# Two output tiles of a streamed projection by turns in two PSUM banks, and the pacing in groups of six

## The chip, the cores and the metric

One core of one Trainium2 chip runs the whole program. The metric is device time in microseconds (us). TensorE (PE in the profile) multiplies, VectorE (DVE) and ScalarE (ACT) do the element-wise work, GpSimd (POOL) does a few small things, SyncE (SP) starts most of the transfers.

## The reference

One block of a hybrid model, 512 tokens by 1024 features in float32. A normalized input is projected once, and three mixers (a gated linear recurrence, a delta-rule recurrence, attention) read parts of that projection. Their gated outputs are summed, projected, and a feed-forward layer follows.

```python
h = rms_norm(x, mix_pre_g)
z = h @ w_in                                   # [512, 11200]
zq, zf, zi, zog, zrw, zcq, zckv, zkr, zgate = split(z)
o_hg, o_rw, o_mla = hgrn2(zq, zf, zi, zog), rwkv7(zrw), mla(zcq, zckv, zkr)
g_hg, g_rw, g_mla = split(sigmoid(zgate), 3)
merged = g_hg * (o_hg @ w_branch[0]) + g_rw * (o_rw @ w_branch[1]) + g_mla * (o_mla @ w_branch[2])
x = x + rms_norm(merged @ w_out, mix_post_g)
gate, up = split(rms_norm(x, ffn_pre_g) @ w_ffn_in, 2)
x = x + rms_norm((silu(gate) * up) @ w_ffn_out, ffn_post_g)
```

## The kernel before

**Products in three parts.** Every float32 operand of a large product is split into a high part, rounded to fp32r, and the low part that is left over. A product of two such operands is three matmuls into one PSUM place: high by high (L136, `whD` and `xH`), high weights by low operand (L137, `whD` and `xL`), low weights by high operand (L138, `wlD` and `xH`). `mm3` issues the three.

**Streamed projections.** `stream` makes two output tiles of 128 features by 512 tokens at a time from 256 columns of weights. The weights come in four slabs of two k-tiles each: a transfer to `wsD` (L200), a cast to `whD` on ACT (L204) and a subtraction to `wlD` on DVE (L131 through L205). `whD` and `wlD` have two places each, so a slab's cast waits until the slab two before it has been read for the last time. For each slab the kernel before takes the first output tile with both k-tiles (six matmuls), then the second. Each output tile has one PSUM bank, under the tag `mmD`. In the first 1,020 us the pool of these banks has two places; in the feed-forward layer it has four. A finished tile is read out by `done`: by ACT to `zst` (L236 for the projection, L250 for the gates), by DVE to `th` in the branches (L1104), by ACT and DVE in the feed-forward layer (L1200, L1201, L1205). The next stream's tile can be begun in a bank only when that has been read out.

**What else runs on TensorE.** Up to about 1,020 us the streams are work that fills TensorE's time between the products of the mixers: `pr` (preparation of the delta-rule recurrence), `zus` and `yb` (its steps and their inverses), `ph` (the gated recurrence), `pm`, `pmt`, `pmo` (attention). Those are float32 products without the split, small ones mostly, and each waits for results of DVE, ACT or POOL. `side_by_side` issues products on different rows of the array one after the other; its first product stands at L190, the others at L193, and each of these is only handed out once the one before it has been issued. From 1,020 us on there is only filling work: the output projection and the feed-forward layer (`po` and again `mmD`).

**The order.** A scheduler lays down the order of each engine's instructions when the program is built. `lane(n)` gives what follows a priority: a lower lane goes first when its operands are ready. Each engine then takes its instructions strictly in this order and waits at each for what it needs.

**Pacing.** `pace` (L140) is told the first and the last matmul of a group. It puts a memset of a one-element tile, `token` (L148), on POOL behind the last one, and makes the first matmul of a group wait for the token of the group PACE before. With groups of three and PACE = 5, at most 15 filling matmuls stand in front of a product of a recurrence.

Of the kernel before, what the change touches and what calls it, by code (L numbers as in the profile page):

```python
# [23 lines left out]
S = 512  # L24
# [17 lines left out]
PACE = 5  # L42
SCALE = 192.0 ** -0.5

# columns of the constants array
# [10 lines left out]
def consts_array():  # L56
    """Constants that the shapes alone decide."""
# [15 lines left out]
def masks_array():  # L73
    """Pairs (s, t), both in one block of HB, in the left and the right half of one block of 2m"""
    i, j = np.arange(P) % HB, np.arange(HB)
    c = np.zeros((P, len(HG_LEVELS), HB), np.float32)
    for n, m in enumerate(HG_LEVELS):
        same = (i[:, None] // (2 * m)) == (j[None, :] // (2 * m))
        c[:, n, :] = same & ((i[:, None] // m) % 2 == 0) & ((j[None, :] // m) % 2 == 1)
    return c  # L80


# rows of the table of per-feature vectors: name, rows of 128
# [13 lines left out]
def vecs_array(inputs):  # L97
    """The per-feature vectors side by side, features on partitions"""
# [3 lines left out]
class Kern:  # L102
# [7 lines left out]
    def lane(self, n):  # L110
        """What follows is issued before what is ready in later lanes."""
# [17 lines left out]
    def split_low(self, dst, src, high, eng=None):  # L129
        """The part of src that rounding it to high left over."""  # L130
        (eng or self.nc.vector).tensor_tensor(dst, src, high.bitcast(F32), op=ALU.subtract)  # L131

    def mm3(self, ps, lh, ll, rh, rl, start, stop):
        """One tile of a float32 product from operands that are split exactly in two."""
# [5 lines left out]
    def pace(self, first, last):  # L140
        """Holds back the products that fill the array's time until those PACE groups before are
        done, so that what a recurrence waits for doesn't queue behind many of them."""
# [10 lines left out]
    def load_w(self, pool, src, kts, n, tag, bufs=None, step=None):  # L153
        """Loads a slab [128, kts, n] of weights in parts of `step` k-tiles and splits it; gives a
        function that gives the parts of k-tile k."""
# [18 lines left out]
    def operand(self):  # L174
        """The 16 tiles of a feature-major operand of 1024 features, in two parts"""
        return [[self.t(self.hp, [P, S], f"x{a}{k}", F32R) for k in range(KD)] for a in "HL"]

    def stream_open(self, es):
        """Places of the weights that run through"""
# [5 lines left out]
    def side_by_side(self, calls):  # L185
        """Products on different rows or columns of the array, issued in this order"""
# [8 lines left out]
    def slab(self, src, pool=None, hold=None):  # L195
        """A part [128, kts, n] (2 KB a partition) of weights, split"""
# [12 lines left out]
    def stream(self, src, x, done, toks=slice(0, S), ps=None):  # L209
        """Feature-major products of up to 256 columns of weights; done(j, ps) takes the tiles."""  # L210
# [4 lines left out]
        for k0 in range(0, KD, 2):  # L215
            h, l = self.slab(src[:, k0:k0 + 2])
            for c, p in zip(cols, ps):
                for k in range(2):
                    group = self.mm3(p[:c.stop - c.start, toks], h[:, k, c], l[:, k, c], xh[k0 + k][:, toks],
                                     xl[k0 + k][:, toks], k0 + k == 0, k0 + k == KD - 1)  # L220
                    if self.pacing:
                        self.pace(*group)
# [8 lines left out]
    def dense_z(self, off, n=256, halves=False):  # L231
        """A part of the input projection, feature-major, to DRAM; in halves of the tokens"""
# [13 lines left out]
    def dense_gate(self, n):  # L246
        """Two tiles of tanh of half the gates' logits, to DRAM"""
# [6 lines left out]
    def dense_fm(self, ps, w, x, kts, col=0, toks=slice(0, S)):  # L254
        """ps[feature, token] = sum over kts of w[k][:, feature]^T x[:, k, token]"""
# [6 lines left out]
    def dense_tm(self, ps, w, x, kts, tt, cols):  # L262
        """ps[token, feature] = sum over kts of x[:, kt, token]^T w[:, kt, feature]"""
# [7 lines left out]
    def rstd(self, dst, ss, n, eps, tmp):  # L271
        """dst = (ss / n + eps) ** -0.5"""
# [58 lines left out]
    def to_fm(self, sp, pp, xs, gname, groups, first=False):  # L331
        """Row-normalizes token tiles and lays them out feature-major, in two parts."""
# [25 lines left out]
    def derived(self, sp):  # L358
        """Per-feature vectors that the inputs give."""
# [22 lines left out]
        # lower bound: softmax over the single layer, cumulative sum less the first  # L382
# [25 lines left out]
    def shifted(self, dst, j):  # L408
        """dst = token shift of the recurrence's input tile j"""
# [23 lines left out]
    def rwkv_group(self, g):  # L433
        """Four heads: what the recurrence needs, the inverses, the recurrence"""
# [45 lines left out]
    def rwkv_prep(self, G, p, q):  # L480
# [8 lines left out]
        # decays, from the chunk's end: ep = exp(c - c_end), em its inverse  # L489
        lh, ll = self.lora_w(((H[0], ins["rwkv_w_up"][0, :, f]), (H[1], ins["rwkv_a_up"][0, :, f])))  # L490

        # the two halves of the rows side by side in the array
# [25 lines left out]
        # normalized keys  # L518
# [24 lines left out]
        # in-context learning rates: a = 2 * rate - 1  # L543
# [13 lines left out]
        # scores  # L557
# [16 lines left out]
        # [b|k] token-major  # L574
# [6 lines left out]
        # bonus  # L581
# [7 lines left out]
        # gate  # L589
# [6 lines left out]
        # values, token-major  # L596
# [9 lines left out]
    def rwkv_inverse(self, G, g):  # L606
        """T = (I - L)^-1 for the chunks' strictly lower triangular L, in blocks of 32"""
# [5 lines left out]
        # transposed and in place  # L613
# [17 lines left out]
    def rwkv_merge(self, G, g):  # L631
        """The inverses' blocks off the diagonal"""
# [22 lines left out]
    def rwkv_chain(self, G, g, between):  # L655
# [10 lines left out]
        for c in range(NC):  # L666
# [5 lines left out]
            if 0 < c < NC - 1:  # L672
                # the state as it comes to the end of the next chunk
# [27 lines left out]
        # layer norm over the head  # L701
# [12 lines left out]
        for q in range(2):  # L714
# [9 lines left out]
            for j in range(2):  # L724
                # odd heads have the two chunks of a tile in the other order
# [9 lines left out]
    def hgrn_open(self, es):  # L735
# [3 lines left out]
        # what lies above the diagonal's blocks stays zero  # L739
# [8 lines left out]
    def hgrn_head(self, h):  # L748
# [5 lines left out]
        # decays and keys  # L754
# [8 lines left out]
        # values, token-major  # L763
# [6 lines left out]
        # output gate, doubled  # L770
# [6 lines left out]
        # scores [s, t] inside tiles of 128 tokens: the diagonal first, then pairs whose tokens  # L777
        # lie in the left and right half of a block of 2m, with the decay up to the middle in q
        # and from there on in k; those inside blocks of HB in their own tile at first
# [530 lines left out]
```

## Time and profile before

| | |
|---|---|
| median of 3 runs | 1442.45 us (1441.33 to 1442.66) |
| the profiled execution, first to last instruction | 1441.5 us |
| TensorE busy | 1410.8 us, 9,832 matmuls |
| matmuls of `stream` | 3 x 1,232 and 3 x 64 |
| VectorE, ScalarE, GpSimd busy | 872.7, 631.7, 154.4 us |
| DMA | 194.94 MB, 135 GB/s |

The profile is of one execution; its span lies 0.95 us under the median. Matmuls overlap, and the duration in a row of a matmul holds its way through the array: a 128x512 matmul of 390 ns is followed by the next one 227 ns later. So what a matmul costs TensorE is read from the distance of two starts, not from its duration. A timeline's columns are: start, duration, engine, line, operation, tiles (out<-in), shape, count, and in brackets how long the engine had been idle and for whom. Rows with a count hold several instructions. Lines are those of the kernel before.

### The profile page before, as it was taken

Reading aid. Unit: us, or ns where it says so; the run is one execution under the profiler, and the core shown is the slowest. Engines: PE = TensorE matmul, PEld = TensorE weight load, DVE = VectorE, ACT = ScalarE, POOL = GpSimd, SP = SyncE. Lnnn points to the kernel's source line nnn. Section 1 sums busy time; section 2 is a strip of 40 time slices with the busy share of each in tenths; the row PEclk is TensorE's granted clock in tenths of the full one; section 3 lists DMA queues with packets and bytes.
Section 4 is the critical chain, followed back from the end, with each engine's and each line's share of the span. In section 5 each row is a group of like instructions: output and inputs, shape, how many; then the busy total and the mean of one; then the engine's idle time right before and its main releaser. Section 6 shows DMA issues by size and latency. Waiting matters only on the chain.

```text
span 1441.5 us, 27838 instructions
## 1 busy us (share of the span) xinstructions
PE 1410.8 (98%) x9832; PEld 1116.7 (77%) x9832; DVE 872.7 (61%) x1910; ACT 631.7 (44%) x1266; POOL 154.4 (11%) x1027
## 2 busy tenths in 40 slices
PE   7999999999999999999999999999999999999998
PEld 6777777777777777777877787887788888888886
DVE  5657967867689496874835666655465444443234
ACT  5563555544646346335543455333354333332222
POOL 2110111110212121111111010001010000000000
PEclk9999999999999999999999999999999999999999
DMA  6455453444544444445532456435544333335333
GB/s 204 141 172 153 132 162 98 140 140 132 171 136 142 125 133 133 129 104 173 153 107 78 141 163 183 137 115 177 198 153 139 99 99 96 95 97 159 95 95 110
DMA packets 172459, 194.94 MB, mean 135 GB/s; under 512 B 33056, under 2 KB 125600, under 8 KB 172320
## 3 DMA queue, kind: packets, MB, share of 16 engines
q1 hardware_dynamic: 170928, 190.02, 43.9%
q10 hardware_dynamic: 1392, 3.15, 0.6%
q8 instruction: 78, 1.28, 0.4%
q14 instruction: 61, 0.50, 0.1%
HBM read 151.30 MB, written 41.81 MB: 134 GB/s over the span
## 4 chain that ended last, share of the span: by engine, by line
PE 88%; DMA 5%; DVE 3%; ACT 2%; issue 1%; SPq 0%; POOL 0%; DVEq 0%; POOLq 0%; ACTq 0%
PE mmD L136 19%; PE mmD L138 18%; PE mmD L137 18%; PE po L136 4%; PE po L138 4%; PE po L137 4%; PE pr L193 2%; PE ph L786 1%; DMA zr<-z 1%; PE yb L697 1%; PE pmo L1082 1%; DMA z<-zst 1%; PE pm L136 1%; PE pm L138 1%; PE pm L137 1%
## 5 line engine op out<-in xcount | busy, mean ns | idle before, releaser
L136 PE MATMUL mmD<-xH,whD 128*128 128x512 f32 (+1 forms) x1232 | 489.9, 399 | 5.8 <-ACT whD L204 3.1
L137 PE MATMUL mmD<-xL,whD 128*128 128x512 f32 (+1 forms) x1232 | 474.1, 386 | 0.0
L138 PE MATMUL mmD<-xH,wlD 128*128 128x512 f32 (+1 forms) x1232 | 453.4, 388 | 2.9 <-DVE wlD L131 2.8
L131 DVE TENSOR_TENSOR wlD<-wsD,whD 128x512 fp32r<-128x512 f32 x384 | 263.5, 687 | 306.0 <-ACT whD L204 294.5
L204 ACT CAST whD<-wsD 128x512 fp32r<-128x512 f32 x384 | 237.5, 619 | 454.6 <-PE mmD L137 290.2
L136 PEld LDWEIGHTS mmD<-xH,whD 128*128 128x128 f32 x1232 | 231.5, 188 | 59.2 <-POOL token L148 5.6
L138 PEld LDWEIGHTS mmD<-xH,wlD 128*128 128x128 f32 x1232 | 230.4, 188 | 52.6 <-DVE wlD L131 5.5
L137 PEld LDWEIGHTS mmD<-xL,whD 128*128 128x128 f32 x1232 | 232.4, 189 | 40.9 <-issue 0.9
L148 POOL MEMSET token<- 1x1 f32 x912 | 82.8, 91 | 786.2 <-PE mmD L138 769.6
L138 PE MATMUL po<-whD,fL 128*128 128x512 f32 x176 | 68.3, 390 | 0.0
L137 PE MATMUL po<-wlD,fH 128*128 128x512 f32 x176 | 68.3, 390 | 0.0
L136 PE MATMUL po<-whD,fH 128*128 128x512 f32 x176 | 50.9, 391 | 0.2
L278 POOL TENSOR_TENSOR rrs<-rtm,mhalf 128x1 f32<-128x1 f32 x8 | 4.7, 589 | 405.2 <-DVE rtm L273 368.0
L236 ACT COPY zst<-mmD 128x512 f32<-128x512 f32 x64 | 37.5, 585 | 21.3 <-PE mmD L138 20.9
L621 DVE TENSOR_TENSOR invtmp<-inv 64x30 f32<-64x30 f32 (+14 forms) x120 | 38.8, 323 | 10.2 <-DMA inv<-Ld 7.9
L622 DVE TENSOR_TENSOR inv<-inv,invtmp 64x30 f32<-64x30 f32 (+14 forms) x120 | 38.3, 319 | 1.9
L136 PEld LDWEIGHTS po<-whD,fH 128*128 128x128 f32 x176 | 32.9, 188 | 8.0 <-DVE y L1177 0.6
L138 PEld LDWEIGHTS po<-whD,fL 128*128 128x128 f32 x176 | 33.0, 188 | 7.1
L137 PEld LDWEIGHTS po<-wlD,fH 128*128 128x128 f32 x176 | 33.0, 188 | 7.0
L695 DVE SCALAR_TENSOR_TENSOR PV<-zus,gC,St 64x64 f32<-64x64 f32 x96 | 27.1, 282 | 10.5 <-PE zus L689 7.2
L786 PEld LDWEIGHTS ph<-hq,hk 128*32 128x32 f32 x1536 | 19.5, 111 | 12.6 <-issue 5.4
L786 PE MATMUL ph<-hq,hk 128*32 128x32 f32 x1536 | 27.4, 200 | 0.3 <-DVE hq L791 0.3
(335 smaller groups left out, 2009.0 us busy)
## 6 DMA issues: line engine op xcount, KB each, us to landing
wsD<-in_w_in_dram SPq DMA_DIRECT2D x176, 256.0 KB, 3.0
wsD<-in_w_ffn_in_dram SPq DMA_DIRECT2D x96, 256.0 KB, 2.8
z<-zst SPq DMA_DIRECT2D x63, 256.0 KB, 2.6
wsD<-in_w_branch_dram SPq DMA_DIRECT2D x48, 256.0 KB, 2.7
wsD<-in_w_ffn_out_dram SPq DMA_DIRECT2D x44, 256.0 KB, 2.6
zr<-z SPq DMA_DIRECT2D x26, 256.0 KB, 3.1
gth<-zst SPq DMA_DIRECT2D x24, 256.0 KB, 2.1
th<-gth SPq DMA_DIRECT2D x24, 256.0 KB, 3.6
```

The costliest lines, as they stand in the source:

```text
L131: (eng or self.nc.vector).tensor_tensor(dst, src, high.bitcast(F32), op=ALU.subtract)
L136: first = mm(ps, lhsT=lh, rhs=rh, start=start, stop=False)
L137: mm(ps, lhsT=lh, rhs=rl, start=False, stop=False)
L138: return first, mm(ps, lhsT=ll, rhs=rh, start=False, stop=stop)
L148: token = self.nc.gpsimd.memset(self.token, 0.0).ins
L193: last = c()
L204: nc.scalar.copy(h, st)
L236: self.nc.scalar.copy(st[:m], ps)
L621: V.tensor_tensor(tv, cv, rv, op=ALU.mult)
L622: V.tensor_tensor(U[:, :j, j + 1:], U[:, :j, j + 1:], tv, op=ALU.add)
L695: V.scalar_tensor_tensor(nxt, zus[H[e], 2, q, :], gc, St[H[e], q, :], op0=ALU.mult, op1=ALU.add)
L786: mm(g[b:b + HB, o // P, :], lhsT=k[:, t], rhs=q[:, t], start=True, stop=True)
```

## The change

In `stream` the loops change places: k-tile by k-tile, and within a k-tile the three kinds of product one after the other, each for both output tiles before the next kind. A group of the pacing is now these six matmuls (two banks, three products), and PACE is 3, so that up to 18 of them stand in front of a recurrence, and half as many tokens are made. `stream` issues its matmuls itself, at L222, and no longer through `mm3`. Comments and docstrings were dropped; what stands below `stream` moves down by three lines (L236 is L239, L786 is L789, L1104 is L1107).

```diff
-PACE = 5
+PACE = 3
...
         for k0 in range(0, KD, 2):
             h, l = self.slab(src[:, k0:k0 + 2])
-            for c, p in zip(cols, ps):
-                for k in range(2):
-                    group = self.mm3(p[:c.stop - c.start, toks], h[:, k, c], l[:, k, c], xh[k0 + k][:, toks],
-                                     xl[k0 + k][:, toks], k0 + k == 0, k0 + k == KD - 1)
-                    if self.pacing:
-                        self.pace(*group)
+            for k in range(2):
+                a, b, i = xh[k0 + k][:, toks], xl[k0 + k][:, toks], k0 + k
+                out = [p[:c.stop - c.start, toks] for c, p in zip(cols, ps)]
+
+                made = [nc.tensor.matmul(o, lhsT=w[:, k, c], rhs=x, start=i == 0 and n == 0, stop=i == KD - 1 and n == 2)
+                        for n, (w, x) in enumerate(((h, a), (h, b), (l, a))) for c, o in zip(cols, out)]
+                if self.pacing:
+                    self.pace(made[0], made[-1])
```

The scheduler lays the order down anew, and it moves more than these lines. Numbers behind a tile's name tell places apart; they differ between the two programs (`mmD_1029` before stands where `mmD_965` stands now).

TensorE, at a product of the delta-rule recurrence (`pr`, the scores of one pair of heads, eight products side by side) within a stream. Before:

```order
L138 MATMUL mmD_1029<-xH_7_106,wlD_1034 128x512
L190 MATMUL pr_4924<-X_775_4679,BK_4907 128x128
L136 MATMUL mmD_1029<-xH_8_107,whD_1055 128x512
L137 MATMUL mmD_1029<-xL_16_115,whD_1055 128x512
L193 MATMUL pr_4925<-X_776_4680,BK_4907 128x128
L193 MATMUL pr_4924<-X_775_4679,BK_4907 128x128
L193 MATMUL pr_4925<-X_776_4680,BK_4907 128x128
```

And now the same eight products:

```order
L222 MATMUL mmD_966<-xL_18_117,whD_1009 128x512
L770 MATMUL ph_7411<-cst,hz_7409 128x128
L789 MATMUL ph_7424<-hq_7407,hk_7401 32x32 x16
L190 MATMUL pr_4564<-X_775_4319,BK_4547 128x128
L193 MATMUL pr_4565<-X_776_4320,BK_4547 128x128
L193 MATMUL pr_4564<-X_775_4319,BK_4547 128x128
L193 MATMUL pr_4565<-X_776_4320,BK_4547 128x128
```

The first of the eight stood alone between filling matmuls, and two of these ran before the other seven; now the eight follow one another, behind products of the gated recurrence. Counted over the whole order, a first product (L190) stood alone in this way 17 times before and stands so twice now. Unbroken stretches of other work between filling matmuls were 293 and are 253.

TensorE, where one stream of the last branch ends and the next begins (no mixer has work left there). Before:

```order
L138 MATMUL mmD_12062<-oH_1809_10879,wlD_12133 128x512
L136 MATMUL mmD_12063<-oH_1808_10878,whD_12132 128x512
L137 MATMUL mmD_12063<-oL_1816_10886,whD_12132 128x512
L138 MATMUL mmD_12063<-oH_1808_10878,wlD_12133 128x512
L136 MATMUL mmD_12063<-oH_1809_10879,whD_12132 128x512
L137 MATMUL mmD_12063<-oL_1817_10887,whD_12132 128x512
L138 MATMUL mmD_12063<-oH_1809_10879,wlD_12133 128x512
L136 MATMUL mmD_12168<-oH_1802_10872,whD_12172 128x512
```

And now:

```order
L222 MATMUL mmD_11631<-oH_1809_10455,wlD_11695 128x512
L222 MATMUL mmD_11630<-oH_1809_10455,whD_11694 128x512
L222 MATMUL mmD_11630<-oL_1817_10463,whD_11694 128x512
L222 MATMUL mmD_11630<-oH_1809_10455,wlD_11695 128x512
L222 MATMUL mmD_11728<-oH_1802_10448,whD_11732 128x512
L222 MATMUL mmD_11728<-oL_1810_10456,whD_11732 128x512
```

`mmD_12168` and `mmD_11728` are begun in the bank of `mmD_12062` and `mmD_11630`. Six matmuls stood between the last one into the old tile and the first into the new one; now none stands there. At the other ends of streams mostly one filling matmul stands there, where mostly four or six did, and with it whatever of the mixers the scheduler found ready; at six of the 55 ends in the first 1,020 us that is nothing.

ACT, where the fourth stream ends and the fifth begins. Before (`whD_707` is the cast of the fourth stream's last slab, `whD_739` and `whD_761` those of the next stream's first two slabs):

```order
L204 CAST whD_707<-wsD_705 128x512
L204 CAST whD_739<-wsD_737 128x512
L236 COPY zst_727<-mmD_637 128x512
L204 CAST whD_761<-wsD_759 128x512
L236 COPY zst_731<-mmD_638 128x512
```

And now (`whD_669` is the last slab, `whD_699` and `whD_719` the next stream's first two):

```order
L204 CAST whD_669<-wsD_667 128x512
L204 CAST whD_699<-wsD_697 128x512
L552 ACTIVATE a_4346<-a_4346,omka,hka 128x512
L204 CAST whD_719<-wsD_717 128x512
L239 COPY zst_687<-mmD_605 128x512
L239 COPY zst_691<-mmD_606 128x512
```

The copy of the first output tile stood ahead of the cast of the next stream's second slab; now it stands behind it, and that cast takes the place of the old stream's last slab, which TensorE reads until two matmuls before the end. It is so at 43 of the 44 ends of streams that ACT reads out.

More of the change, by code (lines that the diff above doesn't have):

```diff
@@ L209, in stream @@
     def stream(self, src, x, done, toks=slice(0, S), ps=None):
+        nc = self.nc
         xh, xl = x
```

## The prediction

> **What bounds the kernel now.** I read the page first, then what TensorE's matmuls cost by the distance of their starts, then the places where TensorE changes between filling matmuls and a mixer's products, then the ends of the streams.
>
> The page's first part, its chain of waits, and one of the three groups of the streams' matmuls (3 x 1,232, some 3,700):
>
> ```profile
> span 1441.5 us, 27838 instructions
> PE 1410.8 (98%) x9832; PEld 1116.7 (77%) x9832; DVE 872.7 (61%) x1910; ACT 631.7 (44%) x1266; POOL 154.4 (11%) x1027
> ...
> PE 88%; DMA 5%; DVE 3%; ACT 2%; issue 1%; SPq 0%; POOL 0%; DVEq 0%; POOLq 0%; ACTq 0%
> ...
> L137 PE MATMUL mmD<-xL,whD 128*128 128x512 f32 (+1 forms) x1232 | 474.1, 386 | 0.0
> ```
>
> TensorE bounds it: no other engine is busy for two thirds of the span. So the change is worth what it does to the time that TensorE spends per matmul, and to the time in which TensorE, taking its instructions in order, stands still. Two stretches without any mixer, from the busy time by windows, tell what a 128x512 matmul costs (the window and its length, then busy us and count for PE, PEld, DVE, ACT, POOL, then the granted clock):
>
> ```profile
> 1110.00:1300.00 190.00, 190.00 (x840) 157.33 (x839) 81.16 (x122) 61.45 (x104) 0.00 (x0) 1.00 0.34 97
> 1325.00:1425.00 100.00, 99.82 (x438) 81.83 (x437) 29.73 (x44) 26.80 (x49) 0.00 (x0) 1.00 0.31 95
> ```
>
> The first is `mmD`, in which two or three matmuls that follow each other go to the same bank: 190 us / 840 = 0.226 us. The second is `po`, whose order goes through four banks by turns: 100 us / 438 = 0.228 us. Below I use 0.23.
>
> **The change part by part.** *The turns themselves.* One end of a stream, in order of time (144.05 is the last matmul into the first tile, 144.28 the first of the last six into the second):
>
> ```profile
> 143.97 0.64 ACT L507 ACTIVATE lw<-t 128x512 f32<-128x512 f32 x1
> 144.05 0.39 PE L138 MATMUL mmD<-xH,wlD 128*128 128x512 f32 x1
> 144.28 0.39 PE L136 MATMUL mmD<-xH,whD 128*128 128x512 f32 x1
> 144.50 0.58 ACT L236 COPY zst<-mmD 128x512 f32<-128x512 f32 x1
> 144.51 0.39 PE L137 MATMUL mmD<-xL,whD 128*128 128x512 f32 x1
> ...
> 145.19 0.39 PE L137 MATMUL mmD<-xL,whD 128*128 128x512 f32 x1
> ...
> 145.41 0.39 PE L138 MATMUL mmD<-xH,wlD 128*128 128x512 f32 x1
> 145.61 0.62 ACT L204 CAST whD<-wsD 128x512 fp32r<-128x512 f32 x1 [0.53 <-PE mmD L137]
> ...
> 145.73 0.46 PE L786 MATMUL ph<-hq,hk 128*32 128x32 f32 x32
> ...
> 146.12 0.50 PE L136 MATMUL mmD<-xH,whD 128*128 128x512 f32 x1
> 146.14 0.58 ACT L236 COPY zst<-mmD 128x512 f32<-128x512 f32 x1
> ```
>
> 144.05 to 144.28 changes the bank, 144.28 to 144.51 stays in it: 0.23 both. With the two windows that makes the turns worth nothing. An end in which every matmul changes banks with a shared moving operand isn't in the trace; 0.002 us, the difference of the windows, bounds a matmul's change to either side, and for some 3,700 matmuls that is 7 us; I take 0, since 0.18 us of the second window is idle and the rest of the difference is a few records.
>
> The Trainium skill, "TensorE: Matmul & The Clock Gate", section "Back-to-back issue gap", gives about 131 ns per matmul of 512 columns as what a stream of weight loads and matmuls sustains, against 216 ns for a matmul by itself. By it 3,700 matmuls could lose some 350 us; neither of this trace's windows comes near to it, in one bank (0.226) or by turns (0.228). What else could come of it is the third rival.
>
> *Fewer changes between filling matmuls and mixers.* Two places with the scores' products, each in order of time, the first with its first product joined to the others, the second with it apart:
>
> ```profile
> 66.92 0.39 PE L138 MATMUL mmD<-xH,wlD 128*128 128x512 f32 x1
> 67.24 0.37 PE L190 MATMUL pr<-X,BK 64*128 64x128 f32 x1
> ...
> 68.33 0.50 PE L136 MATMUL mmD<-xH,whD 128*128 128x512 f32 x1
> 68.67 0.39 PE L137 MATMUL mmD<-xL,whD 128*128 128x512 f32 x1
> ```
>
> ```profile
> 113.00 0.39 PE L138 MATMUL mmD<-xH,wlD 128*128 128x512 f32 x1
> 113.32 0.48 PE L190 MATMUL pr<-X,BK 64*128 64x128 f32 x2
> 113.73 0.50 PE L136 MATMUL mmD<-xH,whD 128*128 128x512 f32 x1
> 114.07 0.40 PE L137 MATMUL mmD<-xL,whD 128*128 128x512 f32 x1
> 114.39 1.16 PE L193 MATMUL pr<-X,BK 64*128 64x128 f32 x14
> 115.48 0.50 PE L136 MATMUL mmD<-xH,whD 128*128 128x512 f32 x1
> ```
>
> Going in costs 113.32 - 113.00 - 0.23 = 0.09 us, coming back 114.07 - 113.73 - 0.23 = 0.11: 0.20 for any stretch. The product apart takes from 113.00 to 113.73, 0.50 more than a filling matmul, and 0.11 behind it: 0.61. Joined it costs nothing: 66.92 to 68.33 with it is 1.41, 114.07 to 115.48 without it is 1.41 as well. The order has 40 stretches fewer (293 to 253), and 15 of them are such first products (17 to 2). That is 15 x 0.61 = 9.2 and 25 x 0.20 = 5.0: 14.2 us less. It lies on the path, TensorE being the bound. The bounds: all 40 at 0.20 (8.0, if what a product apart waits for is waited for elsewhere) and all at 0.61 (24.4).
>
> *The ends of streams.* How many there are comes from the tiles read out, in the view of the tile `mmD`:
>
> ```profile
> L236 ACT COPY zst<-mmD x64: 565/586/617, 27.8 to 569.6; 128x512 f32<-128x512 f32 x63, 64x512 f32<-64x512 f32 x1
> L250 ACT ACTIVATE zst<-mmD x24: 587/598/602, 585.7 to 815.9; 128x512 f32<-128x512 f32 x24
> L1104 DVE SCALAR_TENSOR_TENSOR th<-th,mmD x24: 677/686/689, 828.9 to 1019.2; 128x512 f32<-128x512 f32 x24
> ```
>
> 112 tiles are 56 streams and 55 changes with two banks. Before, the first tile's copy began 0.45 after its last matmul (144.50) beside six matmuls, and the second's beside the next stream. Now both tiles end together. What that costs without cover is seen once, in the last branch, where only two matmuls happened to stand in between:
>
> ```profile
> 983.97 0.40 PE L138 MATMUL mmD<-oH,wlD 128*128 128x512 f32 x1
> ...
> 984.40 1.29 DVE L1104 SCALAR_TENSOR_TENSOR th<-th,mmD 128x512 f32<-128x512 f32 x2 [1.03 <-PE mmD L138]
> 984.43 0.40 PE L138 MATMUL mmD<-oH,wlD 128*128 128x512 f32 x1
> ...
> 985.24 0.47 PE L136 MATMUL mmD<-oH,whD 128*128 128x512 f32 x1 [0.40 <-DVE th L1104]
> 985.55 0.39 PE L137 MATMUL mmD<-oL,whD 128*128 128x512 f32 x1
> ```
>
> A bank read by DVE is free 985.24 - 983.97 = 1.27 after its last matmul began. With one matmul in between TensorE stands still for 1.27 - 0.46 = 0.81, with none for 1.04; coming back costs 985.55 - 985.24 - 0.23 = 0.08. For ACT the cast comes first: it begins 0.42 after the last matmul that reads its place (145.19 to 145.61), the copy 0.53 later (146.14), takes 0.58, and DVE's first read ending at 985.05 (half of 1.29) says 0.19 from there to TensorE: 1.72. That matmul is now the third from the end, so TensorE has 0.69 of work: 1.03 still, and 0.08.
>
> Six changes have no other work in between: three with ACT (3 x 1.11 = 3.3), one with DVE and one matmul (0.89), two with DVE and none (2 x 1.12 = 2.2), less what 983.97 shows already (1.27 - 0.69 + 0.08 = 0.66): 5.8 us. At the other 49 a mixer's products stand there and run meanwhile. Sixteen products of a head like those at 145.73 cover 146.12 - 145.41 - 0.23 = 0.48; the eight of the scores 1.18. By the order ten changes have about the shorter kind: 0 to 0.55 each, the middle 0.27: 2.7. And ACT can come late, with an instruction of 0.64 (143.97) in front: at 16 changes without spare cover 10.2 at most, of which I take a quarter, 2.6. Together 5.8 + 2.7 + 2.6 = 11.1 us more; bounds 5.8 + 2.7 = 8.5 and 18.7.
>
> *The low weights.* The same view, what TensorE waited for at `mmD`:
>
> ```profile
>   DVE wlD L131: 8.3, 14
>   POOL token L148: 6.9, 10
> ```
>
> `wlD` is now first read by a slab's fifth matmul, not the third, 0.46 later. Weight load and matmul are both counted, so the 8.3 are about 4.1 of the array's time; bounds 0 and 4.1 less; I take 1.5, under half, since DVE's own queue shifts too.
>
> *Pacing.* Behind the last matmul of the awaited group stand four groups of three before, two of six now: 12 matmuls or 2.7 us both times. Half of the tokens go, on an engine that is busy for 11%. The 6.9 us, halved as above, bound it by 3.4 to either side; I take 0.
>
> *The feed-forward layer* has four banks, so a tile's bank is wanted 48 matmuls (11 us) later: 0. If that cover were gone, 22 changes at 0.81 would be 18 us, but nothing takes it.
>
> *The clock.* One window runs at half clock:
>
> ```profile
> 670.00:677.00 7.00, 7.00 (x29) 5.83 (x30) 1.26 (x3) 2.50 (x3) 0.35 (x4) 0.51 0.42 115
> ```
>
> It costs 3.4 us. The order around it changes; it may go, or a second one come: 0, with 3.4 to either side.
>
> The sum: -14.2 + 11.1 - 1.5 = -4.6 us, to a span of 1436.9; with the 0.95 us by which the median of the runs lies over this span, 1437.8.
>
> **The rivals.** *The ends of streams win (slower).* The products in the gaps may themselves wait for ACT instructions queued behind the same cast and two copies, and so cover nothing. If half of the 1.03 us stays at each of the 44 changes read by ACT, that is 22.7, and 2.5 in the branches: 25.1 in place of 11.1, so +9.4: 1451.8. It decides once the ends cost over 15.7 us, 0.29 per change. For it: at 983.97 the wait shows as soon as only two matmuls are in between. Against it: 49 of 55 gaps have other work. Chance 0.22.
>
> *Nothing measurable.* The products that are joined only wait longer in one place for what they waited for in two, so that 40 x 0.20 = 8.0 is saved: -8.0 + 11.1 - 1.5 = +1.6: 1444.0. For it: the mixers' products hang on DVE and ACT. Against it: the two equal 1.41 us. Chance 0.26.
>
> *The turns do speed up the stream.* Matmuls of 256 columns come every 0.12 us:
>
> ```profile
> 25.73 0.28 PE L138 MATMUL mmD<-xH,wlD 128*128 128x256 f32 x1
> 25.84 0.28 PE L136 MATMUL mmD<-xH,whD 128*128 128x256 f32 x1
> ```
>
> So about 2 x 0.12 - 0.227 = 0.013 us is fixed per matmul. If that were a turnaround within a bank, 3,700 x 0.013 = 48 us would go: about 1390. `po`, by turns and not faster, speaks against it. Chance 0.02. That the scheduler undoes the turns is a small matter: neighbours among the streams' matmuls change banks 2,789 times of 3,887, before 921.
>
> **How the numbers follow.** My forecast, 0.50, is 1437.8. A difference under 0.2% (2.9 us) can't be told from none here. Faster by more: the forecast and the third rival, 0.52. Within: 0.26. Slower: 0.22. The range goes down to 14.2 grown half-way to its upper bound (19.3) with the ends at 8.5: -19.3 + 8.5 - 1.5 = -12.3, some 1430; and up to just short of the first rival, 1451.
>
> **What would show it.** Right: 128x512 matmuls still 0.226 apart from 1,110 to 1,300 us; about 40 fewer stretches, L190 rows next to L193 rows; three waits of `mmD` for `zst` and three for `th` of 0.8 to 1.0 us each, and small ones elsewhere; fewer waits for `wlD`. Wrong: distances under 0.22 (third rival); waits for `zst` and `th` of over 16 us in all (first); the same total of TensorE's stops with fewer stretches (second).

## The result, and the profile after

The changed kernel takes 1458.28 us (median of 4 runs, 1455.52 to 1460.03); the kernel before, on the same chip, 1442.14 (4 runs, 1441.33 to 1442.66). The ratio is 1.0103 (95% interval 1.0088 to 1.0118): slower by 13 to 17 us, where I forecast 1437.8 and a range that ended at 1451. The profiled execution of the changed kernel took 1455.52 us, the lowest of the four, so the accounts below explain 12.2 of the 16 us between the medians.

The page of the changed kernel, its first part and two groups of the fifth:

```profile
span 1453.7 us, 26881 instructions
PE 1409.2 (97%) x9832; PEld 1121.2 (77%) x9832; DVE 869.0 (60%) x1910; ACT 632.2 (43%) x1266; POOL 114.7 (8%) x571
...
L222 PE MATMUL mmD<-xH,whD 128*128 128x512 f32 (+1 forms) x1232 | 421.7, 397 | 14.3 <-ACT zst L239 11.4
...
L148 POOL MEMSET token<- 1x1 f32 x456 | 41.3, 91 | 790.6 <-PE mmD L222 783.2
```

TensorE's busy time is the same within 2 us, in a span 12.2 us longer: it stands still more. The row of L222 is what to notice. L222 is now the streams' matmul, and at its first form TensorE waited 11.4 us for `zst`, the read-out of a bank; before, the same wait was 1.1 us.

Where in the program? The busy time by windows, cut at the end of the last branch's streams; first the two windows of before, then those of the changed kernel (columns as in the prediction's windows):

```profile
0.00:1019.20 1019.20, 999.45 (x7929) 775.36 (x7930) 689.96 (x1617) 489.99 (x1010) 147.48 (x1014) 1.00 0.48 142
1019.20:1441.50 422.30, 411.34 (x1905) 341.36 (x1903) 182.71 (x294) 141.75 (x257) 6.91 (x13) 1.00 0.38 118
```

```profile
0.00:1032.70 1032.70, 998.17 (x7929) 779.92 (x7930) 687.52 (x1616) 490.04 (x1010) 107.86 (x559) 0.99 0.47 141
1032.70:1453.70 421.00, 411.03 (x1904) 341.25 (x1903) 181.50 (x295) 142.20 (x257) 6.81 (x12) 1.00 0.38 118
```

The same 7,929 matmuls take 13.5 us longer up to there; output projection and feed-forward layer take 1.3 less. In the first part TensorE is idle for 1032.70 - 998.17 = 34.5 us, before 1019.20 - 999.45 = 19.8. And a part of its busy time is at half clock. These windows of the changed kernel have 0.50 in the column of the granted clock:

```profile
218.00:221.40 3.40, 3.40 (x10) 2.61 (x9) 1.15 (x2) 3.32 (x7) 0.09 (x1) 0.50 0.72 213
392.10:395.50 3.40, 3.40 (x10) 2.62 (x9) 2.08 (x3) 2.46 (x4) 0.00 (x0) 0.50 0.93 293
491.10:497.90 6.80, 6.79 (x74) 5.67 (x75) 1.55 (x4) 1.15 (x2) 0.00 (x0) 0.50 0.46 148
```

13.6 us at half clock lose 6.8; before it was 6.8 us (the one at 670) and 3.4. So the account of the first part is +14.8 idle, +3.4 half clock, and the rest of the busy time -4.7: +13.5.

What TensorE waited for, the longest groups of the changed kernel (us in total, times, longest):

```profile
PE mmD L222 <- ACT zst L239: 11.4, 11, 2.6
PE tr L355 <- DVE xn L349: 7.5, 2, 7.1
PE yb L700 <- DVE PV L688: 2.5, 1, 2.5
...
PE mmD L222 <- DVE th L1107: 1.0, 3, 0.6
PE mmD L222 <- ACT zst L253: 0.9, 3, 0.5
```

And of before, the rows of the streams' matmuls:

```profile
PE mmD L138 <- DVE wlD L131: 2.8, 5, 1.0
...
PE mmD L136 <- ACT zst L236: 1.1, 1, 1.1
...
PE mmD L136 <- DVE th L1104: 0.4, 1, 0.4
```

The changed kernel's three rows of `mmD` and a read-out are 13.3 us at 17 places, before's two 1.5 at 2. What such a place looks like, TensorE and ScalarE from 211.3 us on:

```profile
212.22 0.61 PE L222 MATMUL mmD<-xH,wlD 128*128 128x512 f32 x2
212.77 0.46 PE L789 MATMUL ph<-hq,hk 128*32 128x32 f32 x32
...
214.28 0.73 PE L193 MATMUL pr<-wa,lh 64*128 64x512 f32 x3
214.62 0.62 PE L193 MATMUL pr<-wa,ll 64*128 64x512 f32 x2
216.90 0.47 PE L222 MATMUL mmD<-xH,whD 128*128 128x512 f32 x1 [1.66 <-ACT zst L239]
```

```profile
214.92 0.72 ACT L416 ACTIVATE v<-zr,omm 128x512 f32<-128x512 f32 x1 [3.67 <-DMA grw<-v]
215.54 0.60 ACT L204 CAST whD<-wsD 128x512 fp32r<-128x512 f32 x1
216.17 1.07 ACT L239 COPY zst<-mmD 128x512 f32<-128x512 f32 x2
```

The stream's last matmuls run at 212.2. There is other work behind them, over 2 us of it, far more than the 1.03 that I thought an end needs. Yet the copies begin at 216.17, since ScalarE takes its instructions in order and stood 3.67 us at a mixer's instruction (L416) until a transfer had freed its place; the cast and both copies are queued behind that. TensorE stops 1.66 us, and 1 us after it goes on the half clock of 218.0 begins.

The other two stretches at half clock, 10.2 of the 13.6 us, don't follow a read-out. They come within 1.1 us of waits of the mixers' own products for VectorE:

```profile
391.00 0.33 PE L700 MATMUL yb<-PV,LM 64*64 64x64 f32 x2 [2.46 <-DVE PV L688]
491.11 1.11 PE L193 MATMUL yb<-lsq,LM 32*32 32x32 f32 x34 [1.52 <-DVE lsq L644]
```

And the two longest waits for a read-out, 2.56 us up to 31.09 and 1.81 up to 69.47, have no half clock behind them.

### The profile page after: what moved, and what is told of

Its sections match the earlier page's. It is cut to its first block, busy times and chain, and to the rows that moved or that the text cites. A ratio compares the mean times of both kernels' runs of the same rounds, so it can differ in the third digit from the quotient of the medians.

```text
span 1453.7 us, 26881 instructions
## 1 busy us (share of the span) xinstructions
PE 1409.2 (97%) x9832; PEld 1121.2 (77%) x9832; DVE 869.0 (60%) x1910; ACT 632.2 (43%) x1266; POOL 114.7 (8%) x571
## 3 DMA queue, kind: packets, MB, share of 16 engines
q8 instruction: 78, 1.28, 0.4%
## 4 chain that ended last, share of the span: by engine, by line
PE 58%; DMA 4%; DVE 3%; ACT 1%; issue 1%; SPq 0%; POOL 0%; DVEq 0%; POOLq 0%; ACTq 0%
PE mmD L222 35%; PE po L136 4%; PE po L138 3%; PE po L137 3%; PE pmo L1085 1%; PE pm L136 1%; PE pm L137 1%; PE pm L138 1%; DMA lnx<-grw 1%; PE pm L1069 1%; DMA wsD<-in_w_out_dram 1%; PE pmt L1081 1%; DVE wlD L131 1%; PE yb L700 1%; DMA Td<-inv 0%
## 5 line engine op out<-in xcount | busy, mean ns | idle before, releaser
L222 PE MATMUL mmD<-xH,whD 128*128 128x512 f32 (+1 forms) x1232 | 421.7, 397 | 14.3 <-ACT zst L239 11.4
L222 PE MATMUL mmD<-xL,whD 128*128 128x512 f32 (+1 forms) x1232 | 408.8, 387 | 0.0
L222 PE MATMUL mmD<-xH,wlD 128*128 128x512 f32 (+1 forms) x1232 | 406.4, 389 | 0.1
L222 PEld LDWEIGHTS mmD<-xH,whD 128*128 128x128 f32 x1232 | 226.7, 189 | 67.7 <-issue 16.3
L222 PEld LDWEIGHTS mmD<-xH,wlD 128*128 128x128 f32 x1232 | 226.9, 189 | 47.4 <-DVE wlD L131 0.6
L222 PEld LDWEIGHTS mmD<-xL,whD 128*128 128x128 f32 x1232 | 229.1, 189 | 43.7 <-issue 1.0
L148 POOL MEMSET token<- 1x1 f32 x456 | 41.3, 91 | 790.6 <-PE mmD L222 783.2
L239 ACT COPY zst<-mmD 128x512 f32<-128x512 f32 x64 | 34.2, 587 | 0.6 <-DMA Ld<-LM 0.2
L698 DVE SCALAR_TENSOR_TENSOR PV<-zus,gC,St 64x64 f32<-64x64 f32 x96 | 27.1, 283 | 10.6 <-PE zus L692 8.5
L789 PEld LDWEIGHTS ph<-hq,hk 128*32 128x32 f32 x1536 | 18.7, 111 | 13.6 <-issue 5.6
L678 POOL TENSOR_TENSOR St<-PV,gC 64x128 f32<-64x128 f32 x48 | 22.9, 476 | 67.4 <-DVE PV L698 56.8
```

Source lines behind the costliest of these rows:

```text
L148: token = self.nc.gpsimd.memset(self.token, 0.0).ins
L222: made = [nc.tensor.matmul(o, lhsT=w[:, k, c], rhs=x, start=i == 0 and n == 0, stop=i == KD - 1 and n == 2) for n, (w, x) in enumerate(((h ...
L239: self.nc.scalar.copy(st[:m], ps)
L678: nc.gpsimd.tensor_tensor(St[H[e]], PV[e][H[e], :, c, :], gC[H[e], :, c + 1:c + 2].to_broadcast([64, 2, C]), op=ALU.mult)
L698: V.scalar_tensor_tensor(nxt, zus[H[e], 2, q, :], gc, St[H[e], q, :], op0=ALU.mult, op1=ALU.add)
```

## The experiments

Theory A: the loss is made at the ends of the streams, where both read-outs come together and late. Theory B: the pacing (18 matmuls in front in place of 15, half the tokens) makes it. Theory C, which came up after the first four runs: the order of before happens to have few stops, and any edit that has the whole front part laid anew brings some. Each run is put beside the kernel before on the same chip; at the end a table has the accounts of all of them.

**The pacing alone.** Before's loop, with one token for the six matmuls of a tile's slab, and PACE 3:

```diff
-                    group = self.mm3(...)
-                    if self.pacing:
-                        self.pace(*group)
+                    made += self.mm3(...)
+                if self.pacing:
+                    self.pace(made[0], made[-1])
```

> The kernel before with the change's pacing alone: groups of six matmuls (one output tile, two k-tiles), PACE 3, no turns. Its order has 288 stretches of other work (293 before) and 12 lone first products (17). Theory A (the ends of the streams cost what was lost): ends are as before, so 5 x 0.61 less, 1439 to 1442 us. Theory B (the pacing costs: 18 matmuls in front of a recurrence, half the tokens): most of the 16 us, 1453 or more.

1466.97 us, ratio 1.0163 (1.0134 to 1.0192): slower than the whole change. Theory A can't explain this run, since its ends are those of before, one tile after the other. Late read-outs show here all the same, 7.0 us at 6 places where before has 1.5 at 2.

**The turns alone**, with a token for each three matmuls and PACE 5:

```diff
-                    self.pace(made[0], made[-1])
+                    self.pace(made[0], made[2])
+                    self.pace(made[3], made[-1])
```

> The turns alone: the changed loop, but groups of three matmuls and PACE 5. Order: 283 stretches, 7 lone first products, at 35 ends of streams one filling matmul between the last into the old tile and the first into the new, at 20 ends two. Theory A: the ends cost about 20 us as in the change (two matmuls in between take a little off), 10 x 0.61 less for the lone products: about 1456 (1450 to 1460). Theory B: as fast as before or a little faster, 1436 to 1442.

1461.19 us, ratio 1.0135 (1.0114 to 1.0156), 1 us over the range of A. But its streams waited 5.9 us for read-outs, less than half of the 13.3 of the changed kernel, and more of its loss is half clock (10.2 us in the table below). And this +18 and the +24 of the pacing are 42 together, where both at once cost 16: they aren't terms of a sum.

**The changed kernel with the last slab of each stream one tile after the other**, so that the first tile's read-out is under way while six matmuls of the second run:

```diff
+            if k0 == KD - 2:
+                for c, p in zip(cols, ps):
+                    made = []
+                    for k in range(2):
+                        made += self.mm3(p[...], h[:, k, c], l[:, k, c], ...)
+                    if self.pacing:
+                        self.pace(made[0], made[-1])
+                continue
```

> The change, but the last slab of each stream tile by tile again: all six matmuls into the first output tile, then six into the second, so that the first tile's bank is read out beside the second tile's last six. Turns in three slabs of four, groups of six, PACE 3. Order: 278 stretches, 8 lone. Theory A: the ends cost nothing again, 9 x 0.61 + 6 x 0.20 = 6.7 less than before: about 1435 (1433 to 1441). Theory B: the loss stays, 1453 or more.

1452.35 us, ratio 1.0076 (1.0053 to 1.01). The waits of a stream for a read-out are down to those of before (1.5 us in all), and some 6 of the 16 us are gone; 10 stay. Neither theory alone.

**The turns in the feed-forward layer only**, where nothing is paced; ahead of the `continue` stands before's loop, and PACE is 5:

```diff
+            if self.pacing:
+                ...
+                continue
+            for k in range(2):
+                ...
+                made = [nc.tensor.matmul(o, ...) for ... for c, o in zip(cols, out)]
```

> The turns in the feed-forward layer alone, where four banks are there and no pacing; the first 1,020 us as before (same order, 293 stretches). Theory A and B: 1442 (1440.5 to 1443.5), since 128x512 matmuls come every 0.227 us in one bank and by turns. A third theory (turns slow the array or the read-out there): 1,056 matmuls at a few ns more, 1445 or more.

1443.05 us, ratio 0.9999 (0.9988 to 1.001). Here the front part keeps its order, and nothing is lost or won: turning between banks is free there, to within the 1.7 us of the interval, and where a bank isn't wanted at once the ends are too.

**Turns in three slabs, the last apart, the tokens and PACE of before**: neither the ends nor the pacing differ from before, only the body of the stream.

> Turns in the first three slabs of each stream, the last slab one tile after the other, groups of three and PACE 5 as before: the ends of the streams and the pacing are those of before, only the body of the stream goes by turns. Theory A (the loss comes from the ends of the streams, where both read-outs come together): 1438 to 1446 us. Theory B (the loss comes from 18 matmuls in front and half the tokens): also 1438 to 1446. Theory C (before's order is one in which TensorE rarely stops, and any edit that has the order laid anew brings stops of 6 to 15 us and half-clock stretches behind them): 1450 to 1466.

1450.53 us, ratio 1.0067 (1.0047 to 1.0087). A and B both fail; it is at the lower end of C's range. The run doesn't tell whether the new order costs this or the turns in the body themselves, by what they make wait elsewhere.

**PACE 6 with groups of three** (`PACE = 6`, nothing else):

> Before's loop with PACE 6 in place of 5: 18 matmuls in front, but in groups of three, with as many tokens as before, and no turns. Theory A: 1440 to 1445, since the ends are as before. Theory B with 18 in front as the cause: about 1466, as with groups of six and PACE 3; with the coarser groups as the cause: 1442. Theory C: 1448 to 1466.

1449.26 us, ratio 1.0055 (1.0039 to 1.0072): 8 us, a third of what groups of six and PACE 3 cost with the same 18 in front.

**Groups of six with PACE 2** (the first experiment with `PACE = 2`):

> Before's loop in groups of six with PACE 2: 12 matmuls in front where before has 15, half the tokens, no turns. Theory A: 1440 to 1446. Theory B with 18 in front as the cause: 1440 to 1446; with the coarser groups as the cause: about 1466. Theory C: 1448 to 1466.

1456.7 us, ratio 1.0115 (1.0093 to 1.0137). Fewer in front and still slower by 16: the number in front isn't the cause either. Nor is the size of the groups by itself: with 18 in front groups of six cost 16 us more than groups of three, with 12 (1459.03, below) about the same.

**The changed kernel without the wait for read-outs:**

```diff
-            self.nc.scalar.copy(st[:m], ps)
+            c = self.nc.scalar.copy(st[:m], self.h[0][0][:m].bitcast(F32))
+            self.tc.add_manual_dep(c.ins, self.last, ...)
```

and the same for the tanh of the gates.

> The changed kernel, but the 64 copies and 24 tanh of the projections read a tile in SBUF in place of the PSUM bank, still only after the stream's last matmul: what they write is not the projection, and no stream waits for a read-out in a branch's front part. Theory A: the 17.6 us that TensorE stood before 20 read-outs go, and some 3 us of half clock: 1437 to 1444. Theories B and C: the pacing and the newly laid order stay, 1450 to 1458.

1447.49 us, ratio 1.0047 (1.0031 to 1.0063). Neither A's range came (1437 to 1444) nor that of B and C (1450 to 1458). Beside the kernel before on its own chip this is +6.3 us, the changed kernel +16.1. So the read-outs' share of the change is about 10 us by the medians, 8 by the ratios, and some 6 us stay without them. The order is newly laid here once more, and newly laid orders differ by as much (+8 to +24 in these runs), so this run alone can't fix the share.

**Another order alone.** The kernel before with one priority changed (loads and decays of the gated recurrence ahead of the delta-rule preparation in place of behind it), no turns, no other pacing:

```diff
-        self.lane(6)
+        self.lane(4.5)
```

> The kernel before with one number changed: HGRN's loads and decays get priority lane 4.5 in place of 6, ahead of RWKV's preparation in place of behind it. Streams, products, pacing and read-outs are those of before; the whole front part is laid in another order. Theory A (ends of streams) and theory B (the pacing's numbers): 1438 to 1445 us. Theory C (the order of before is one with few stops, and one laid anew has more of them): 1447 to 1458, with 4 to 7 gaps of over 1.3 us between TensorE's starts where before has 3, and 5 to 10 us of half clock lost in place of 3.4.

1451.29 us, ratio 1.0062 (1.0042 to 1.0082), from an edit that touches no stream and no token. It does move one mixer's work ahead of another's, so it isn't a new order and nothing else; ScalarE, too, has 18 table loads here in place of 16. The time is what C expected; the way is only partly: three gaps of over 1.3 us as before, not 4 to 7, but more at half clock, here

```profile
193.20:200.00 6.80, 6.80 (x69) 5.58 (x64) 5.11 (x9) 3.60 (x6) 0.36 (x4) 0.50 0.59 177
483.30:486.70 3.40, 3.40 (x24) 2.27 (x24) 1.08 (x5) 1.34 (x3) 0.26 (x3) 0.50 0.70 230
664.20:667.60 3.40, 3.40 (x11) 2.82 (x12) 2.93 (x11) 2.17 (x3) 0.09 (x1) 0.50 0.43 132
```

13.6 us of it in place of 6.8, and 3.9 us more of busy time.

**The second tile read out by VectorE**, in the changed kernel:

```diff
-            self.nc.scalar.copy(st[:m], ps)
+            (self.nc.vector.tensor_copy if j else self.nc.scalar.copy)(st[:m], ps)
```

> The changed kernel with the second tile of each projection read out by VectorE and the first by ScalarE, so that two read-outs need not stand one behind the other on ScalarE. Theory A: part of the 13.3 us before read-outs goes, as far as ScalarE was the one held up: 1446 to 1453. If VectorE is as late as ScalarE was: 1456 to 1462. Theory C: what the ends give back, stops elsewhere take, 1450 to 1462.

1461.18 us, ratio 1.013 (1.0096 to 1.0165). The waits of a stream for a read-out fall from 13.3 to 9.3 us (2.9 of these now for VectorE's copies), but TensorE's other waits for VectorE grow from 17.1 to 21.0 us: nothing is left of it. A mend at one place is taken back elsewhere, as C says; that VectorE would be as late as ScalarE (1456 to 1462) fits as well.

**The changed kernel with PACE 2:**

> The changed kernel with PACE 2 in place of 3: 12 matmuls in front. Theory A: 10 ends without any work between them where the changed kernel has 6, so 1458 to 1466. Theory B with 18 in front as the cause: 1444 to 1452. Theory C: anywhere from 1447 to 1466.

1471.78 us, ratio 1.0197 (1.0159 to 1.0234), the slowest of all, and over every theory's range: 40.7 us idle and 37.5 us at half clock, which lose 18.8. Its streams waited only 5.4 us for read-outs; the half clock is what sets it apart.

**PACE 4 with groups of three:**

> Before's loop with PACE 4 in place of 5: 12 matmuls in front, groups of three, no turns. Theory A: 1440 to 1446. Theory B with 18 in front as the cause: 1436 to 1442, since fewer stand in front. Theory C: 1447 to 1460, as for PACE 6, and more stretches (315 for 294) add some 4 us of starts anew.

1459.03 us, ratio 1.0108 (1.0082 to 1.0133). This is in C's range alone. PACE 5 is the best of the three, 4 and 6 both lose.

The accounts of the front part, each up to the end of the last branch's streams (window, idle, and half of the time at half clock; "rest" is the busy time without that loss; differences to before). Each row is one profiled execution, which can lie off the median of its kernel: that of the pacing alone 6.4 us under, that of the changed kernel with two read out 5.8 over.

```
kernel                      end      idle   half clock   rest    sum
before                    1019.2     19.8      3.4      996.0
changed                   +13.5    +14.8     +3.4      -4.7   +13.5
pacing alone              +17.8    +10.4     +5.1      +2.3   +17.8
turns alone               +14.6     +8.4    +10.2      -4.0   +14.6
last slab apart            +9.7     +6.3     +3.4       0.0    +9.7
turns in feed-forward      -0.2     +1.2     -1.7      +0.3    -0.2
turns in the body         +11.8     +5.4     +5.1      +1.3   +11.8
PACE 6, threes             +6.6     +2.3     +1.7      +2.6    +6.6
PACE 2, sixes             +14.5     +7.8     +8.5      -1.8   +14.5
changed, no read-out       +2.1     +5.8      0.0      -3.7    +2.1
another order alone        +8.9     +1.6     +3.4      +3.9    +8.9
changed, two read out     +23.7    +18.2     +5.1      +0.4   +23.7
changed, PACE 2           +33.6    +20.9    +15.4      -2.7   +33.6
PACE 4, threes            +11.1     +5.8     +1.7      +3.6   +11.1
```

Four rows of it, from the windows of the pacing alone, of the turns alone, of the changed kernel without read-outs and of the other order:

```profile
0.00:1037.00 1037.00, 1006.83 (x7929) 779.38 (x7930) 690.79 (x1618) 497.78 (x1014) 108.18 (x558) 0.99 0.46 140
```

```profile
0.00:1033.80 1033.80, 1005.66 (x7929) 781.95 (x7930) 687.83 (x1616) 491.47 (x1012) 147.80 (x1014) 0.99 0.47 140
```

```profile
0.00:1021.30 1021.30, 995.74 (x7929) 775.80 (x7930) 686.65 (x1616) 488.37 (x1010) 109.35 (x559) 1.00 0.47 142
```

```profile
0.00:1028.10 1028.10, 1006.76 (x7929) 778.91 (x7930) 692.22 (x1617) 493.63 (x1012) 146.54 (x1014) 0.99 0.46 141
```

Where TensorE waits, by the idle times that the timelines give, counted from the sixth matmul before the end of a stream to the second one of the next: 23.9, 14.8, 17.8 and 20.1 us in the four kernels in which both tiles end together and are read out (changed, turns alone, two read out, PACE 2), 4.8 in the one without read-outs, 1.8 before, and 2.0 to 6.7 in the eight others. Of the 23.9, 13.3 are the streams' waits for read-outs and 10.6 those of the mixers' products in the gaps, for VectorE and GpSimd, where before these were 0.3. At all other places it waits for 17.8 us before, 10.2 in the changed kernel, 13.1 with the turns alone, and 18.7 to 23.4 in the other eleven. So theory A's loss is there wherever both tiles end together; what the other runs lose is idle time elsewhere, half clock and busy time.

Every kernel in which the front part was laid anew has more idle time, and all but one more time at half clock. What makes the stops looked at here is alike: an engine that works in order is held up, and what TensorE needs next is queued behind it. Here is the largest one of the pacing alone, whose ends are as before. ScalarE's instructions ahead of TensorE's matmul at 167.08, which waited 2.73 us for `zst`:

```profile
160.12 1.28 ACT L758 ACT_TABLE_LOAD   x1
161.41 0.63 ACT L758 ACTIVATE hk<-hf 128x512 f32<-128x512 f32 x1
162.06 1.28 ACT L515 ACT_TABLE_LOAD   x1
163.36 0.64 ACT L515 ACTIVATE cs<-lw 128x520 f32<-128x520 f32 x1
163.90 0.62 ACT L516 ACTIVATE em<-lw 128x520 f32<-128x520 f32 x1
164.54 1.28 ACT L759 ACT_TABLE_LOAD   x1
165.83 0.63 ACT L759 ACTIVATE hf<-hf 128x512 f32<-128x512 f32 x1
166.37 0.57 ACT L237 COPY zst<-mmD 128x512 f32<-128x512 f32 x1
```

Two mixers' functions stand here by turns, and each change loads a table for 1.28 us: 20 loads in this kernel, 16 before and in the changed one. And the largest one of the turns alone, where a mixer's product is wanted 4.51 us before VectorE has its operand, which is queued behind one (L778) that hangs on a ScalarE instruction (L777), and that waits for its load:

```profile
195.38 0.63 PE L222 MATMUL mmD<-xH,wlD 128*128 128x512 f32 x2
200.52 0.66 PE L790 MATMUL ph<-hq,hk 128*32 128x32 f32 x32 [4.51 <-DVE hq L795]
```

```profile
194.03 0.60 ACT L204 CAST whD<-wsD 128x512 fp32r<-128x512 f32 x1
198.31 0.63 ACT L777 ACTIVATE hsg<-hz 128x512 f32<-128x512 f32 x1 [3.68 <-DMA hz<-z]
198.97 0.69 DVE L778 SCALAR_TENSOR_TENSOR hsg<-hsg,hz 128x512 f32<-128x512 f32 x1 [3.47 <-ACT hsg L777]
```

No order that beats before's came up, and no run points to one. Not tried: the turns with the order of before held as it was.

## Why the prediction was wrong

The account in the terms of the forecast: the ends of streams +22.1 us for +11.1 (waits 23.9, before 1.8); fewer stretches and low weights together -12.3 for -15.7 (busy time -4.7, waits elsewhere -7.6); the clock +3.4 for 0. With 0.3 us of smaller gaps that is +13.5 for -4.6.

*The turns themselves, 0:* right. From 1,120 to 1,300 us the changed kernel's matmuls are as far apart as before, in banks by turns with a shared moving operand:

```profile
1120.00:1300.00 180.00, 180.00 (x796) 149.05 (x795) 75.59 (x116) 59.06 (x99) 0.00 (x0) 1.00 0.34 97
```

180 / 796 = 0.226 us, and the feed-forward experiment gives 0.9999. The third rival is out. The 0.226 us also speak against the sentence on 131 ns quoted there from the Trainium skill.

*Fewer stretches, -14.2:* not settled, but near. TensorE's busy time without the half clock fell by 4.7 us, and its waits away from the ends by 7.6, of which 2.8 are those for `wlD`: 4.7 + 7.6 - 2.8 = 9.5 us without these. Fits of the stretches' times by their contents, made on the trace of before and laid over the changed kernel's, give 3 to 9 us less, depending on how they are made, and the starts anew are 23.8 us before and 19.6 after. That is argued from traces; no run isolates it.

*The ends of streams, +11.1 (8.5 to 18.7):* **this is the step that failed.** TensorE's waits for read-outs rose by 11.8 us (1.5 to 13.3), which alone would have been my number, in part by luck: at the six places without other work ScalarE's three took 2.56, 1.81 and 1.06 us, where I had 1.11 for each, and VectorE's three 1.0 in all, where I had 3.1. But the mixers' products in the gaps, which I took to run meanwhile, wait there themselves: 10.6 us for VectorE and GpSimd, as at 391.00 and 491.11, where before they waited 0.3 at ends. Together +22.1, near the 25.1 of the first rival, which said that the products in the gaps may cover nothing; the engine that it named was ScalarE. Three things were missing in the working. I asked whether a gap holds enough other work to cover a read-out that starts on time; what decides is when it starts, and both copies and the cast stand in ScalarE's queue behind mixers' instructions that wait for transfers (3.67 us at 211). I had allowed a quarter of 0.64 us x 16 for that. Where no filling matmul can be begun, nothing covers the waits of the mixers' products. And a stop can be followed by a stretch at half clock.

In the run without read-outs both are mostly gone: its waits for read-outs are 1.2 us (the branches keep theirs) and those of the products in the gaps 3.5. But its waits elsewhere are 20.5 us in place of 10.2, so that on the clock 8 to 10 us are won and not 19. Why VectorE and GpSimd are late at the ends, whether by the copies and casts or by what the scheduler put there, is open.

*What no step held: a new order.* I counted gains and losses only where the edit is. Six runs with the ends as before and a newly laid front part cost 8 to 24 us (the other order alone 9, turns in the body 9, the pacings 8 to 24). In the changed kernel 6 us stay without the read-outs. That those are this same effect is the likeliest reading, since nothing of the edit but turns and pacing is left there; it isn't shown for each of them. A rival is open: the priorities and PACE of the kernel before may have been chosen because they do well, so that any step away from them loses; that is no cost of a new order as such, and no run here starts from another order. The range should have held the loss all the same: no trace of before tells its size.

*Pacing, 0 (3.4 to either side):* wrong by itself (PACE 4 and 6, groups of six: all slower, by 8 to 24 us), though it is no separate term of the change, since the turns with the old pacing are as slow (1461.19) as with the new.

*Low weights, -1.5:* right or better. The row of 2.8 us in which TensorE waited for `wlD` is gone, and in the view of the tile `mmD` the wait that was 8.3 us, 14 times, is

```profile
  DVE wlD L131: 0.6, 2
```

*Feed-forward layer, 0:* right, 422.3 and 421.0 us for all that follows the branches. *Clock, 0 (3.4 to either side):* at its bound, +3.4. My test for the first rival, waits for `zst` and `th` of over 16 us in all, was wrong too: they were 13.3, since the waits of the products in the gaps stand in other rows.

## What to carry to other kernels

Where a scheduler lays the order of several engines, price an edit to the busiest stream with a term for the new order itself, and take it from control runs: change a priority or a pacing number that the edit doesn't need, and time it. Here one priority moved the time by 0.6%, and six edits that left the ends of streams as they were by 0.6 to 1.6%, so one run shows that there is such a term, and several its range. For a read-out that must come before the next fill, ask what is queued ahead of it on its engine and what that waits for, and whether the work in the gap waits itself, rather than how much of it there is. And effects of stops don't add: the turns (+18) and the pacing (+24) gave 16 together.

## What the runs showed of the hardware

TensorE's granted clock drops to half for stretches of 3.4 or 6.8 us (once each 10.2 and 13.7), most of them close to a short stop. In the front parts of the 14 kernels, from 35 us on, 38 starts of matmuls came 1.7 us or more after the one before; in 26 of them a stretch at half clock began within 5.5 us of the stop's beginning, in all four of over 3 us; of 36 gaps of 1.3 to 1.7 us, in 8. No run sets a stop by itself, so this is a count and not a rule. The Trainium skill, "TensorE: Matmul & The Clock Gate", section "HAM oscillation — how this bites in real kernels", gives idle gaps of over about 3.4 us as the rule; by these runs half of that, from start to start, is often enough. 11 of the 44 stretches came without any of these gaps, as at 670 us in before.

A change between the two mixers' ScalarE functions loads a table for 1.28 us, and how often that happens (14 to 20 times here) follows from the order.
